# An up projection by seven block products in place of eight, in a phase of its own, in a hybrid encoder layer

## The chip, the cores and the metric

The kernel runs on one core of a Trainium2 chip. Times are device microseconds. Five engines work from queues of their own: PE (matmul; its weight loads are shown as PEld), DVE (vector), ACT (scalar), POOL (GpSimd), and SP, which here only issues DMAs. Semaphores order what depends on each other. The metric is the time of one execution; 2132.58 us is the median of three runs before the change (2130.88 to 2136.26).

## The reference

One layer, sequence 512, width 2048, all in f32:

```python
h = rms_norm(x, pre_mix_g)
proj = h @ w_in                                  # 2048 -> 1024 + 2 * 1024
y_ssm  = s5_mixer(u, ...)                        # diagonal state space, gelu, GLU
y_conv = conformer_conv_mixer(v, g, ...)         # causal depthwise conv of 31 taps
y = concatenate([y_ssm, y_conv]) @ w_out
x = x + rms_norm(y, post_mix_g)
h = rms_norm(x, pre_ffn_g)
up = causal_depthwise_conv(h @ w_up, conv_w)     # 2048 -> 2 * 5632, 3 taps
gate, val = split(up, 2)
f = (gelu(gate) * val) @ w_down                  # 5632 -> 2048
x = x + rms_norm(f, post_ffn_g)
```

The change is in the last four lines of matmul work: w_up, and the way from there to w_down.

## The kernel before

Everything is held with channels on the 128 partitions and the 512 time steps in the free dimension, so a row of tiles is 128 channels by 512. x has 16 such rows, gate and val 44 each.

**Products in three parts.** For f32 accuracy every weight tile and every activation is split into a high part, rounded to fp32r, and the low rest, and three matmuls are done for each block: high by high (L118), high weight by low activation (L119), low weight by high activation (L120). The right operands are `hl` (high and low of the normalised x). Weights come in pieces of 512 KB as 128x1024 f32 tiles `wraw` (three buffers), by DMAs that SP issues (L88); ACT casts each to `wh` (L98), DVE subtracts to get `wl` (L99), two buffers each. A piece serves 8 blocks, 24 matmuls of 512 columns. `gemm` does four output rows at a time in four PSUM banks of a pool `mm` of six.

**The stages.** Norm, W_in, state space and conv work, W_out (to about 640 us). Then the x-add stage, lines 677 to 698: per row of x, DVE multiplies the new part by the norm (L686, which reads the norm from the PSUM tile `aux`), adds x (L687), ACT makes the high part and DVE the low part of the next operand (L689), POOL adds up squares (L697); x+y goes to DRAM as `x1scr`, for it is needed again at the end.

**The FFN.** `up(i)` makes 2 rows of gate and 2 of val: 8 weight pieces, 192 matmuls; DVE evacuates PSUM times the norm `rr` into padded buffers `ab` (L720); per row of f, ACT does tap 0 (L728), DVE taps 1 and 2 (L730), ACT the gelu (L733), DVE the product of gate and val (L734), ACT and DVE the split into `hidh` and `hidl` (L736, L738), which stay in SBUF. `down(b)` takes four of these rows: 16 output rows, each accumulated in SBUF tiles `s` over the 11 calls (L755). 22 ups and 11 downs alternate. Before the last down, two DMAs of 2 MB bring x1 back (L774) into the `hl` tiles that the ups no longer need. `rsqrt_bcast` (L133, L146) sums squares over the partitions by matmuls of one column and spreads the result by matmuls with a diagonal.

**The order** on each engine is set by a scheduler that goes by program order and by priorities: weight loads and splits are raised by WPRI, evacuations by EPRI. Each engine, and SP's queue, then runs its list strictly in that order.

## Time and profile before

| | us |
|---|---|
| median of 3 runs | 2132.58 (2130.88 to 2136.26) |
| the profiled execution | 2129.79 |
| its span, first to last instruction | 2128.0 |
| PE busy in the span | 2012.5 (95%) |
| DVE, ACT, POOL busy | 1218.9, 666.3, 287.6 |

The span runs from the first to the last instruction of the profiled execution. "Busy" of PE counts pipelined matmuls, whose single times overlap; so the pitch, the time per instruction in a stretch without holes, is what counts there. Where an engine is idle the profile gives the instruction that ended the wait, after an arrow. In the first 700 us the engines take turns at being full, after that PE is busy nearly without a break until 2098 us; the mean granted TensorE clock is 0.976 of 2.4 GHz.

### The profile page before, as it was taken

The numbers are of one execution on the slowest core, as the hardware profiler recorded it, in microseconds if no ns is written. First come the engines' busy times: TensorE is split into PE (matmuls) and PEld (weight loads), VectorE is DVE, ScalarE is ACT, GpSimd is POOL, SyncE is SP. The second block draws the span as 40 slices with busy tenths as digits, with TensorE's granted clock in tenths as the row PEclk, the third lists the DMA queues.
The fourth block names the chain that finished last, engine by engine and source line by source line (L and its number), as shares of the span: only waits on it lengthen the run. The fifth ranks groups of instructions, "written<-read, shape, count | busy, mean of one in ns | idle before, by whom it ended". The sixth has DMA issues, their size and how long they took to land.

```text
span 2128.0 us, 23254 instructions
## 1 busy us (share of the span) xinstructions
PE 2012.5 (95%) x9190; PEld 1654.4 (78%) x9190; DVE 1218.9 (57%) x1609; ACT 666.3 (31%) x827; POOL 287.6 (14%) x291
## 2 busy tenths in 40 slices
...
GB/s 207 184 219 171 187 187 221 85 89 98 169 99 119 110 99 99 99 92 96 99 99 97 92 99 99 99 93 96 99 99 98 92 98 99 99 93 96 99 168 99
DMA packets 111373, 252.36 MB, mean 119 GB/s; under 512 B 28064, under 2 KB 49568, under 8 KB 110752
## 3 DMA queue, kind: packets, MB, share of 16 engines
...
q14 instruction: 37, 0.30, 0.0%
HBM read 229.67 MB, written 21.17 MB: 118 GB/s over the span
## 4 chain that ended last, share of the span: by engine, by line
PE 72%; DVE 3%; ACT 1%; issue 0%; DVEq 0%; ACTq 0%
PE mm L120 24%; PE mm L118 24%; PE mm L119 24%; DVE hl L689 0%; DVE s L779 0%; DVE s L686 0%; DVE wl L99 0%; DVE hidh L687 0%; PE aux L146 0%; DVE s L780 0%; DVE hidl L687 0%; ACT L139 0%; ACT wh L98 0%; ACT tmp L763 0%; ACT tmp L659 0%
## 5 line engine op out<-in xcount | busy, mean ns | idle before, releaser
L99 DVE TENSOR_TENSOR wl<-wraw,wh 128x1024 fp32r<-128x1024 f32 (+1 forms) x353 | 447.6, 1268 | 772.1 <-ACT wh L98 766.1
L118 PE MATMUL mm<-hl,wh 128*128 128x512 f32 x2112 | 832.7, 395 | 23.3 <-ACT wh L98 14.6
L119 PE MATMUL mm<-hl,wh 128*128 128x512 f32 x2112 | 831.8, 394 | 0.2 <-DVE hl L689 0.2
L120 PE MATMUL mm<-hl,wl 128*128 128x512 f32 x2112 | 777.5, 396 | 52.5 <-DVE wl L99 52.5
L98 ACT CAST wh<-wraw 128x1024 fp32r<-128x1024 f32 (+1 forms) x353 | 370.7, 1050 | 1077.6 <-PE mm L119 1006.3
L120 PEld LDWEIGHTS mm<-hl,wl 128*128 128x128 f32 x2112 | 402.5, 191 | 148.1 <-DVE wl L99 64.1
L118 PEld LDWEIGHTS mm<-hl,wh 128*128 128x128 f32 x2112 | 402.8, 191 | 108.6 <-ACT wh L98 15.4
L119 PEld LDWEIGHTS mm<-hl,wh 128*128 128x128 f32 x2112 | 402.7, 191 | 86.4 <-DVE hl L689 1.4
L119 PE MATMUL mm<-hidl,wh 128*128 128x512 f32 x704 | 273.8, 389 | 0.0
L118 PE MATMUL mm<-hidh,wh 128*128 128x512 f32 x704 | 273.2, 389 | 0.0
L120 PE MATMUL mm<-hidh,wl 128*128 128x512 f32 x704 | 252.6, 389 | 0.0
L765 POOL TENSOR_TENSOR ssq<-ssq,tmp 128x512 f32<-128x512 f32 x11 | 17.4, 1583 | 1380.6 <-ACT tmp L763 1380.0
L571 DVE SCALAR_TENSOR_TENSOR csb<-z,c_conv_w,csb 128x512 f32<-128x512 f32 x210 | 181.0, 920 | 0.0
L118 PEld LDWEIGHTS mm<-hidh,wh 128*128 128x128 f32 x704 | 132.1, 188 | 27.9 <-ACT wh L98 0.5
L120 PEld LDWEIGHTS mm<-hidh,wl 128*128 128x128 f32 x704 | 132.2, 188 | 27.5
L119 PEld LDWEIGHTS mm<-hidl,wh 128*128 128x128 f32 x704 | 132.1, 188 | 27.3
L755 DVE TENSOR_TENSOR s<-mm,s 128x512 f32<-128x512 f32 x160 | 109.3, 690 | 44.4 <-PE mm L120 44.2
L730 DVE SCALAR_TENSOR_TENSOR tmp<-ab,c_ffn_conv_w,tmp 128x512 f32<-128x512 f32 x176 | 125.3, 745 | 0.0
L728 ACT ACTIVATE tmp<-ab,c_ffn_conv_w 128x512 f32<-128x512 f32 x88 | 63.0, 719 | 44.5 <-DVE ab L720 44.5
L720 DVE TENSOR_TENSOR ab<-mm,rr 128x512 f32<-128x512 f32 x88 | 60.3, 688 | 8.2 <-PE mm L120 4.5
L568 POOL TENSOR_TENSOR csb<-csb,pt 128x512 f32<-128x512 f32 x30 | 49.3, 1645 | 60.4 <-ACT pt L567 60.4
L736 ACT CAST hidh<-tmp 128x512 fp32r<-128x512 f32 x44 | 27.2, 621 | 78.1 <-DVE tmp L734 78.1
...
## 6 DMA issues: line engine op xcount, KB each, us to landing
wraw<-in_ffn_w_up SPq DMA_DIRECT2D x176, 512.0 KB, 3.4
wraw<-in_ffn_w_down SPq DMA_DIRECT2D x88, 512.0 KB, 3.4
wraw<-in_w_in SPq DMA_DIRECT2D x47, 512.0 KB, 5.2
wraw<-in_w_out SPq DMA_DIRECT2D x32, 512.0 KB, 3.4
...
k<-in_ssm_bT SPq DMA_DIRECT2D x8, 512.0 KB, 3.7
...
```

The lines of the kernel that those rows point to most:

```text
L98: se.copy(out=h[:, o], in_=raw[:, o])
L99: ve.tensor_tensor(out=l[:, o], in0=raw[:, o], in1=h[:, o].bitcast(F32), op=SUB)
L118: pe.matmul(ps[m], wh[:, kk, m, :], xh, start=k == 0, stop=False)
L119: pe.matmul(ps[m], wh[:, kk, m, :], xl, start=False, stop=False)
L120: pe.matmul(ps[m], wl[:, kk, m, :], xh, start=False, stop=k == nk - 1)
L568: ge.tensor_tensor(out=csb[:, c, :], in0=csb[:, c, :], in1=pt, op=ADD)
L571: ve.scalar_tensor_tensor(out=csb[:, c, :], in0=zk, scalar=w, in1=csb[:, c, :], op0=MUL, op1=ADD)
L720: ve.tensor_tensor(out=t[:, 2:], in0=ps[j], in1=r2, op=MUL)
L728: se.activation(out=o, in_=t[:, 0:S], func=AF.Copy, scale=fcw[:, c, 0:1])
L730: ve.scalar_tensor_tensor(out=o, in0=t[:, k:k + S], scalar=fcw[:, c, k:k + 1], in1=o, op0=MUL, op1=ADD)
L736: se.copy(out=h, in_=cvt[0])
L755: ve.tensor_tensor(out=ft(m), in0=ps[i], in1=ft(m), op=ADD)
```

## The change

Four rows of f are made by `up` as before (`up(0)`, `up(1)`). For the other 40, w_up's part for one row is seen as a 2 by 2 matrix of blocks: gate or val (index 1 or 2) by lower or upper half of the contraction, each block a 128x1024 tile (w11, w12, w21, w22); h is 2 by 2 as well, contraction half by half of the 512 time steps. The product of two such matrices is made by seven block products in place of eight, after Winograd's form of Strassen's method. The sums of h are made once (`xsum` L757, `xsplit` L761 and L762): t1 = h12 - h11, t2 = h22 - t1, t3 = h22 - h12, t4 = h21 - t2. Those of the weights are made for each row: s1 = w21 + w22 and w11 - w21 on POOL (L805, L808), s1 - w11 and w12 less that on DVE (L841, L848). Each product is split (L787 on ACT, L788 on DVE) and run as 8 x 3 matmuls of 256 columns (L793 to L795). The partial sums are put together on their way from PSUM: two copies on ACT, five additions of 256 columns on DVE (L818, L822, L845, L853, L854); the multiplication by the norm (L819, L823) and that of gate and val (L732) are POOL's. A row's last two products, t4 and 22, are done after the first of the next row. `wh` and `wl` have three buffers.

f goes to DRAM (`fscr`, L733). After the whole up phase the down phase reads it back four rows at a time (`fload`: L876, cast L878, low part L880). For the sums, ACT makes a second scaled copy of all 16 rows of h in f32 (L702). The rows of x are loaded into tiles of their own. The reload of x1 is now L915.

```diff
+NP = 4
+HS = S // 2
...
+    for k in range(DK):
+        x1 = xip.tile([P, S], F32, name=f"xin{k}")
+        sy.dma_start(out=x1, in_=a["x"][:, k, :])
+        x1s.append(x1)
...
     x1scr = dram.tile([P, DK, S], F32, name="x1scr")
-    x1s = []
-    for k in range(DK):
-        x1 = hid.tile([P, S], F32, name="hidl" if k % 2 else "hidh")
-        sy.dma_start(out=x1, in_=a["x"][:, k, :])
-        x1s.append(x1)
+    fscr = dram.tile([P, NFF, S], F32, name="fscr")
...
     r2 = rsqrt_bcast([xs2], D)
...
+    for k in range(DK):
+        se.activation(out=yt(k), in_=x1s[k], func=AF.Copy, scale=g2[:, k:k + 1])
...
+    tset = [[xt.tile([P, 8, HS], F32R, name=f"t{i}{p}") for p in "hl"] for i in range(3)]
+    NA = 4
+    abuf = [xt.tile([P, S + 2], F32, name=f"ab{i}") for i in range(NA)]
...
+    def gated(f, ab, mul):
+        cvt = []
...
+            se.activation(out=o, in_=t[:, 0:S], func=AF.Copy, scale=fcw[:, c, 0:1])
+            for k in (1, 2):
+                ve.scalar_tensor_tensor(out=o, in0=t[:, k:k + S], scalar=fcw[:, c, k:k + 1], in1=o,
+                                        op0=MUL, op1=ADD)
+            cvt.append(o)
+        se.activation(out=cvt[0], in_=cvt[0], func=AF.Gelu_apprx_tanh)
+        mul.tensor_tensor(out=cvt[0], in0=cvt[0], in1=cvt[1], op=MUL)
+        sy.dma_start(out=fscr[:, f, :], in_=cvt[0])
...
                 ve.tensor_tensor(out=t[:, 2:], in0=ps[j], in1=r2, op=MUL)
             ab.append(t)
...
-            se.activation(out=cvt[0], in_=cvt[0], func=AF.Gelu_apprx_tanh)
-            ve.tensor_tensor(out=cvt[0], in0=cvt[0], in1=cvt[1], op=MUL)
-            h = hid.tile([P, S], F32R, name="hidh")
-            se.copy(out=h, in_=cvt[0])
-            l = hid.tile([P, S], F32R, name="hidl")
-            ve.tensor_tensor(out=l, in0=cvt[0], in1=h.bitcast(F32), op=SUB)
-            hrow.append((h, l))
+            gated(2 * i + f, ab[2 * f:2 * f + 2], ge)
+
+    up(0)
...
+    q11, q12 = yo[0][:, :, 0:HS], yo[0][:, :, HS:S]
+    q21, q22 = yo[1][:, :, 0:HS], yo[1][:, :, HS:S]
+    xset = {"11": (hh[0][:, :, 0:HS], hl_[0][:, :, 0:HS]), "21": (hh[1][:, :, 0:HS], hl_[1][:, :, 0:HS]),
+            "22": (hh[1][:, :, HS:S], hl_[1][:, :, HS:S]), "t4": (hh[0][:, :, HS:S], hl_[0][:, :, HS:S])}
+    for i in range(3):
+        xset[f"t{i + 1}"] = tuple(tset[i])
+
+    def xsum(name, dst, in0, in1):
+        ve.tensor_tensor(out=dst, in0=in0, in1=in1, op=SUB)
+
+    def xsplit(name, src):
+        h, l = xset[name]
+        se.copy(out=h, in_=src)
+        ve.tensor_tensor(out=l, in0=src, in1=h.bitcast(F32), op=SUB)
+
+    xsum("t1", q11, q12, q11)
+    xsplit("t1", q11)
+    xsum("t3", q12, q22, q12)
+    xsum("t2", q22, q22, q11)
+    xsplit("t2", q22)
+    xsplit("t3", q12)
+    xsum("t4", q21, q21, q22)
+    for i in range(1, NP // 2):
+        up(i)
+    xsplit("t4", q21)
+    s16x.close()
+
...
+    def product(raw, name, ps, first, last):
+        pool = sp if nw[0] % 3 == 2 else wp
+        nw[0] += 1
+        h = pool.tile([P, 1024], F32R, name="wh")
+        l = pool.tile([P, 1024], F32R, name="wl")
+        with tc.high_priority(offset=WPRI):
+            se.copy(out=h, in_=raw)
+            ve.tensor_tensor(out=l, in0=raw, in1=h.bitcast(F32), op=SUB)
+        h, l = (v.rearrange("p (k f) -> p k f", f=P) for v in (h, l))
+        xh_, xl_ = xset[name]
+        o = ps[:, 0:HS]
+        for k in range(8):
+            pe.matmul(o, h[:, k, :], xh_[:, k, :], start=first and k == 0, stop=False, skip_group_check=True)
+            pe.matmul(o, h[:, k, :], xl_[:, k, :], start=False, stop=False, skip_group_check=True)
+            pe.matmul(o, l[:, k, :], xh_[:, k, :], start=False, stop=last and k == 7, skip_group_check=True)
+
+    def quad_load(f):
+        src = a["ffn_w_quad"][f - NP]
+        with tc.high_priority(offset=WPRI):
+            w21 = sp.tile([P, 1024], F32, name="rb", bufs=4)
+            sy.dma_start(out=w21, in_=src[2])
+            w22 = sp.tile([P, 1024], F32, name="rb", bufs=4)
+            sy.dma_start(out=w22, in_=src[3])
+            s1 = sp.tile([P, 1024], F32, name="s1", bufs=2)
+            ge.tensor_tensor(out=s1, in0=w21, in1=w22, op=ADD)
+            w11 = wp.tile([P, 1024], F32, name="wraw", bufs=3)
+            sy.dma_start(out=w11, in_=src[0])
+            ge.tensor_tensor(out=w21, in0=w11, in1=w21, op=SUB)
+            w12 = wp.tile([P, 1024], F32, name="wraw", bufs=3)
+            sy.dma_start(out=w12, in_=src[1])
+        return w11, w12, w21, w22, s1
+
+    def quad_end(f, st_):
+        (w11, w12, w21, w22, s1), ab, (px, py, pz) = st_
+        gate, val = ab
+        product(w22, "t4", py, False, True)
+        with tc.high_priority(offset=EPRI):
+            ve.tensor_tensor(out=val[:, 2:2 + HS], in0=py[:, 0:HS], in1=val[:, 2:2 + HS], op=ADD)
+            ge.tensor_tensor(out=val[:, 2:], in0=val[:, 2:], in1=r2, op=MUL)
+        product(w12, "22", pz, False, True)
+        with tc.high_priority(offset=EPRI):
+            ve.tensor_tensor(out=gate[:, 2 + HS:], in0=pz[:, 0:HS], in1=gate[:, 2 + HS:], op=ADD)
+            ge.tensor_tensor(out=gate[:, 2:], in0=gate[:, 2:], in1=r2, op=MUL)
+        gated(f, ab, ge)
+
+    before = None
+    for f in range(NP, NFF):
+        ws = quad_load(f)
+        w11, w12, w21, w22, s1 = ws
+        ab = [anext(), anext()]
+        gate, val = ab
+        px = psm.tile([P, S], F32, name="mm")
+        product(w11, "11", px, True, False)
+        with tc.high_priority(offset=EPRI):
+            se.copy(out=val[:, 2:2 + HS], in_=px[:, 0:HS])
+        if before:
+            quad_end(f - 1, before)
+        pz = psm.tile([P, S], F32, name="mm")
+        product(s1, "t1", pz, True, False)
+        with tc.high_priority(offset=WPRI):
+            ve.tensor_tensor(out=s1, in0=s1, in1=w11, op=SUB)
+        py = psm.tile([P, S], F32, name="mm")
+        product(s1, "t2", py, True, False)
+        with tc.high_priority(offset=EPRI):
+            ve.tensor_tensor(out=gate[:, 2 + HS:], in0=py[:, 0:HS], in1=val[:, 2:2 + HS], op=ADD)
+        product(w12, "21", px, False, True)
+        with tc.high_priority(offset=WPRI):
+            ve.tensor_tensor(out=w12, in0=w12, in1=s1, op=SUB)
+        with tc.high_priority(offset=EPRI):
+            se.copy(out=gate[:, 2:2 + HS], in_=px[:, 0:HS])
+        product(w21, "t3", py, False, False)
+        with tc.high_priority(offset=EPRI):
+            ve.tensor_tensor(out=val[:, 2 + HS:], in0=py[:, 0:HS], in1=val[:, 2:2 + HS], op=ADD)
+            ve.tensor_tensor(out=val[:, 2 + HS:], in0=pz[:, 0:HS], in1=val[:, 2 + HS:], op=ADD)
+        before = (ws, ab, (px, py, pz))
+    quad_end(NFF - 1, before)
+    spx.close()
...
+    def fload(b):
+        r = []
+        for i in range(4):
+            t = hid.tile([P, S], F32, name="fin", bufs=6)
+            sy.dma_start(out=t, in_=fscr[:, 4 * b + i, :])
+            h = hid.tile([P, S], F32R, name="hidh")
+            se.copy(out=h, in_=t)
+            l = hid.tile([P, S], F32R, name="hidl")
+            ve.tensor_tensor(out=l, in0=t, in1=h.bitcast(F32), op=SUB)
+            r.append((h, l))
+        return r
+
+    def down(b, rhs):
         for g in range(4):
-            ps = gemm(a["ffn_w_down"][b, g], hrow[4 * b:4 * b + 4])
+            ps = gemm(a["ffn_w_down"][b, g], rhs)
...
-    for i in range(NFF // 2):
-        up(i)
-        if i >= 2 and i % 2 == 0:
-            down(i // 2 - 1)
-    x1r = [hl16.tile([P, 8, S], F32, name="hl") for _ in range(2)]
-    for i in range(2):
-        sy.dma_start(out=x1r[i], in_=x1scr[:, 8 * i:8 * i + 8, :])
-    down(NB - 1)
+    nxt = fload(0)
+    for b in range(NB):
+        rhs = nxt
+        if b + 1 < NB:
+            nxt = fload(b + 1)
+        if b == NB - 1:
+            x1r = [hl16.tile([P, 8, S], F32, name="hl") for _ in range(2)]
+            for i in range(2):
+                sy.dma_start(out=x1r[i], in_=x1scr[:, 8 * i:8 * i + 8, :])
+        down(b, rhs)
...
+    r["ffn_w_quad"] = wu.reshape(2, 8, P, 2, NFF, P).transpose(4, 3, 0, 2, 1, 5)[NP:].reshape(NFF - NP, 4, P, 8 * P)
```

On DVE, one stretch of an up phase before: `wl` are weight splits, `ab` evacuated rows, `tmp` convolution results, `hid` the operands for down.

```order
L730 SCALAR_TENSOR_TENSOR tmp_9051<-ab1_5215,c_ffn_conv_w_472,tmp_9051 128x512
L99 TENSOR_TENSOR wl_9112<-wraw_9109,wh_9111 128x1024
L730 SCALAR_TENSOR_TENSOR tmp_9061<-ab2_5216,c_ffn_conv_w_472,tmp_9061 128x512
L734 TENSOR_TENSOR tmp_9047<-tmp_9047,tmp_9051 128x512
L730 SCALAR_TENSOR_TENSOR tmp_9065<-ab3_5217,c_ffn_conv_w_472,tmp_9065 128x512
L730 SCALAR_TENSOR_TENSOR tmp_9061<-ab2_5216,c_ffn_conv_w_472,tmp_9061 128x512
L730 SCALAR_TENSOR_TENSOR tmp_9065<-ab3_5217,c_ffn_conv_w_472,tmp_9065 128x512
L738 TENSOR_TENSOR hidl_9059<-tmp_9047,hidh_9057 128x512
L99 TENSOR_TENSOR wl_9142<-wraw_9139,wh_9141 128x1024
L734 TENSOR_TENSOR tmp_9061<-tmp_9061,tmp_9065 128x512
L738 TENSOR_TENSOR hidl_9073<-tmp_9061,hidh_9071 128x512
L99 TENSOR_TENSOR wl_9172<-wraw_9169,wh_9171 128x1024
```

Splits stand one by one between the work on the two rows of f that the last `up` has made.

And in the change, one row of f (s1, rb, wraw: weight blocks or their sums):

```order
L845 TENSOR_TENSOR ab0_5231<-mm_10970,ab1_5232 128x256
L788 TENSOR_TENSOR wl_11073<-wraw_11066,wh_11072 128x1024
L788 TENSOR_TENSOR wl_11102<-rb_10830,wh_11101 128x1024
L853 TENSOR_TENSOR ab1_5232<-mm_10970,ab1_5232 128x256
L854 TENSOR_TENSOR ab1_5232<-mm_10940,ab1_5232 128x256
L788 TENSOR_TENSOR wl_11132<-wraw_10837,wh_11131 128x1024
L788 TENSOR_TENSOR wl_11174<-s1_11064,wh_11173 128x1024
L841 TENSOR_TENSOR s1_11064<-s1_11064,wraw_11066 128x1024
L818 TENSOR_TENSOR ab1_5232<-mm_10970,ab1_5232 128x256
L788 TENSOR_TENSOR wl_11204<-s1_11064,wh_11203 128x1024
L822 TENSOR_TENSOR ab0_5231<-mm_10940,ab0_5231 128x256
L788 TENSOR_TENSOR wl_11233<-wraw_11069,wh_11232 128x1024
```

The splits are seven per row of f where they were four, two combinations (L841, L848) and the five short evacuations join them; the product and the low part of f are gone from here, the four convolution steps (L728, most of them in the rows left out) are the same.

On POOL before, nothing stands between the x-add stage (L697) and the last call of down (L765). In the change, these five repeat for every one of the 40 rows of f:

```order
L805 TENSOR_TENSOR s1_8512<-rb_8508,rb_8510 128x1024
L808 TENSOR_TENSOR rb_8508<-wraw_8514,rb_8508 128x1024
L819 TENSOR_TENSOR ab1_5232<-ab1_5232,rr_5203 128x512
L823 TENSOR_TENSOR ab0_5231<-ab0_5231,rr_5203 128x512
L732 TENSOR_TENSOR tmp_8377<-tmp_8377,tmp_8381 128x512
```

Two operations on weights, two on evacuated rows (`ab`), one on f now stand in one queue; the first two are for the row two after the one to which the others belong.

On SP before, the reload of x1 into `hl` behind the last weights of up:

```order
L88 DMA wraw_13927<-in_ffn_w_up 128x1024
L88 DMA wraw_13957<-in_ffn_w_up 128x1024
L774 DMA hl_14019<-x1scr_5029 128x4096
L774 DMA hl_14020<-x1scr_5029 128x4096
L88 DMA wraw_14027<-in_ffn_w_down 128x1024
L88 DMA wraw_14057<-in_ffn_w_down 128x1024
L88 DMA wraw_14109<-in_ffn_w_down 128x1024
```

Weights of down come after it, and nothing of f passes this queue.

And in the change, at the end of the up phase (`fin` is f coming back):

```order
L733 DMA fscr_5054<-tmp_14873 128x512
L90 DMA wraw_15206<-in_ffn_w_down 128x1024
L90 DMA wraw_15236<-in_ffn_w_down 128x1024
L915 DMA hl_18070<-x1scr_5053 128x4096
L915 DMA hl_18071<-x1scr_5053 128x4096
L90 DMA wraw_15274<-in_ffn_w_down 128x1024
L876 DMA fin_15086<-fscr_5054 128x512
L876 DMA fin_15092<-fscr_5054 128x512
L876 DMA fin_15098<-fscr_5054 128x512
L733 DMA fscr_5054<-tmp_15064 128x512
L876 DMA fin_15104<-fscr_5054 128x512
```

The reload stands behind four weight pieces of down, and ahead of the fifth and of the first loads of f; the store of the last row of f (L733) is among these loads.

## Rows read from the trace of the kernel before

**Rows 1.** Windows: busy us and instructions per engine, clock, DMA share, GB/s.
```profile
650.00:700.00 50.00, 42.32 (x165) 32.43 (x164) 49.33 (x54) 25.47 (x38) 23.46 (x15) 0.90 0.39 137
1200.00:1400.00 200.00, 200.00 (x884) 165.66 (x883) 83.93 (x97) 48.23 (x53) 0.00 (x0) 1.00 0.30 98
2100.00:2128.00 28.00, 5.94 (x33) 4.96 (x31) 20.36 (x37) 5.68 (x9) 10.30 (x8) 0.63 0.39 150
```

**Rows 2.** Page, costliest groups: busy, mean ns; idle before, its releaser.
```profile
L120 PE MATMUL mm<-hl,wl 128*128 128x512 f32 x2112 | 777.5, 396 | 52.5 <-DVE wl L99 52.5
```

**Rows 3.** Groups by form, 860 to 2100 us: DVE and ACT.
```profile
L99 DVE TENSOR_TENSOR wl<-wraw,wh 128x1024 fp32r<-128x1024 f32 x227 | 278.8, 1228 | 611.3 <-ACT wh L98 611.3
...
L98 ACT CAST wh<-wraw 128x1024 fp32r<-128x1024 f32 x227 | 239.3, 1054 | 770.5 <-PE mm L119 770.5
...
L730 DVE SCALAR_TENSOR_TENSOR tmp<-ab,c_ffn_conv_w,tmp 128x512 f32<-128x512 f32 x152 | 108.5, 745 | 0.0
...
L728 ACT ACTIVATE tmp<-ab,c_ffn_conv_w 128x512 f32<-128x512 f32 x76 | 54.7, 719 | 40.3 <-DVE ab L720 40.3
...
L733 ACT ACTIVATE tmp<-tmp 128x512 f32<-128x512 f32 x38 | 23.6, 621 | 0.0
```

**Rows 4.** Groups by form, whole span: POOL.
```profile
L697 POOL TENSOR_TENSOR ssq<-ssq,tmp 128x512 f32<-128x512 f32 x15 | 23.5, 1564 | 48.9 <-ACT tmp L696 48.8
...
L244 POOL TENSOR_TENSOR cf<-cf,cx 128x256 f32<-128x256 f32 x2 | 1.5, 731 | 0.0
...
L244 POOL TENSOR_TENSOR k<-k,sm_coi 128x512 f32<-128x512 f32 x1 | 1.1, 1062 | 0.0
```

**Rows 5.** Timeline, x-add stage: DVE (start, us, line, names).
```profile
655.06 1.41 DVE L687 TENSOR_TENSOR hidh<-hidh,s 128x512 f32<-128x512 f32 x1
...
657.05 0.67 DVE L686 TENSOR_TENSOR s<-s,aux 128x512 f32<-128x512 f32 x1
...
658.25 1.78 DVE L689 SCALAR_TENSOR_TENSOR hl<-hidh,c_pre_ffn_g,hl 128x512 fp32r<-128x512 f32 x1
...
672.39 2.32 DVE L99 TENSOR_TENSOR wl<-wraw,wh 128x1024 fp32r<-128x1024 f32 x1
```

**Rows 6.** Timeline, the same stretch: POOL.
```profile
654.64 1.28 POOL L697 TENSOR_TENSOR ssq<-ssq,tmp 128x512 f32<-128x512 f32 x1 [28.70 <-ACT tmp L696]
657.89 1.60 POOL L697 TENSOR_TENSOR ssq<-ssq,tmp 128x512 f32<-128x512 f32 x1 [1.97 <-ACT tmp L696]
...
672.03 1.60 POOL L697 TENSOR_TENSOR ssq<-ssq,tmp 128x512 f32<-128x512 f32 x1 [1.97 <-ACT tmp L696]
```

**Rows 7.** Chain that ended last: start, share of the chain in us.
```profile
656.47 0.66 DVE hl L689
657.13 0.60 DVE s L686
...
667.09 1.14 DVE wl L99
...
700.31 0.79 PE aux L133 x8
...
706.93 0.89 PE aux L146 x8
```

**Rows 8.** DMA issues: KB each, median us to landing; then line L88's own.
```profile
wraw<-in_ffn_w_down SPq DMA_DIRECT2D x88, 512.0 KB, 3.4
...
hl<-x1scr SPq DMA_DIRECT2D x2, 2048.0 KB, 11.9
...
DMA to landing us min/median/max: 3.3/3.4/11.1
```

**Rows 9.** Windows round an idle stretch of PE, columns as in rows 1.
```profile
97.90:109.50 11.60, 0.00 (x0) 0.00 (x0) 4.87 (x8) 0.13 (x1) 0.00 (x0) 0.60 1.03 207
109.50:115.50 6.00, 5.97 (x17) 4.79 (x18) 6.00 (x10) 0.23 (x1) 0.00 (x0) 0.64 1.19 224
115.50:120.00 4.50, 4.50 (x75) 3.74 (x74) 0.92 (x2) 1.98 (x3) 0.05 (x1) 1.00 1.04 410
```

More of the change, by code (lines that the diff above doesn't have):

```diff
@@ L123, in layer_kernel @@
     gpre = cload("pre_mix_g", [P, DK], se)
-    ones = const.tile([P, P], F32, name="ones")
+    ones = constr.tile([P, P], F32, name="ones")
     ge.memset(ones, 1.0)
@@ L698, in layer_kernel @@
     r2 = rsqrt_bcast([xs2], D)
-    fa = [s16.tile([P, 8, S], F32, name="s16") for _ in range(2)]
-    def ft(m):
-        return fa[m // 8][:, m % 8, :]
-    NA = 6
-    abuf = [t2.tile([P, S + 2], F32, name=f"ab{i}", bufs=1) for i in range(NA)]
+    for k in range(DK):
+        se.activation(out=yt(k), in_=x1s[k], func=AF.Copy, scale=g2[:, k:k + 1])
+    xin.close()
+    upx = ExitStack()
+    xt = upx.enter_context(tc.tile_pool(name="xt", bufs=1, reuse_waits="tile"))
+    tset = [[xt.tile([P, 8, HS], F32R, name=f"t{i}{p}") for p in "hl"] for i in range(3)]
+    NA = 4
+    abuf = [xt.tile([P, S + 2], F32, name=f"ab{i}") for i in range(NA)]
     for t in abuf:
@@ L710, in layer_kernel, with anext @@
     na = [0]
-    hrow = []
+    def anext():
+        t = abuf[na[0] % NA]
+        na[0] += 1
+        return t
+    def gated(f, ab, mul):
+        cvt = []
+        for j in range(2):
+            c = f + NFF * j
+            t = ab[j]
+            o = tmp()
+            se.activation(out=o, in_=t[:, 0:S], func=AF.Copy, scale=fcw[:, c, 0:1])
[6 more added lines that the diff above has]
+        sy.dma_start(out=fscr[:, f, :], in_=cvt[0])
     def up(i):
@@ L716, in up @@
         for j in range(4):
-            t = abuf[na[0] % NA]
-            na[0] += 1
+            t = anext()
             with tc.high_priority(offset=EPRI):
```

50 lines of the change are left out of this document (24 added, 26 removed).

## The prediction

> **What bounds the kernel now.** I read the table of windows first. From 700 us on PE has no hole: in 1200 to 1400 it is busy 200.00 of 200 us with 884 matmuls, one per 0.2262 us, at granted clock 1.00, while DVE stands at 83.93, ACT at 48.23 and POOL at nothing [rows 1]. So in the FFN only the number and pitch of the matmuls count: a row of f (gate and value, 96 matmuls of 512 columns) is 96 x 0.2262 = 21.72 us, and the down part is 2112 x 0.2262 = 477.8 us. Before 700 us other engines rule, in 650 to 700 DVE (49.33 of 50 us); after 2100 PE is nearly idle [rows 1]. The list of groups says the same: of PE's waits the largest is 52.5 us for wl in 2112 matmuls [rows 2]; a busy 200 of 200 leaves none of it to the later FFN. The profiled execution took 2129.79 us, its span 2128.0, so 1.8 us lie around the span; it is 2.8 us below the median of 2132.58.
>
> **The change part by part.**
>
> *Products.* Rows 0 to 3 of f keep the old form. Each of the other 40 becomes 7 x 8 x 3 = 168 matmuls of 256 columns: 7/8 of the columns, but 1.75 times the instructions and weight loads. No 256-column matmul stands in the trace. Half of 0.2262 is 0.113, which is the low end. Of the 0.2262, 0.2133 is 512 columns at 2.4 GHz; if the other 0.013 is per instruction, a half is 0.1067 + 0.013 = 0.120. Does the weight load fit under it? The chain shows eight matmuls of one column, each with its own 128x128 load, in 0.79 us, and eight of 128 columns of f32 in 0.89 [rows 7]: at most 0.11 each, and the load bound is as good as independent of what streams beside it, so load and stream overlap. If they did not, 0.1067 + 0.11 = 0.22 would be the other end. I take 0.120: 168 x 0.120 = 20.2 us per row on PE (18.8 at 0.112), against 21.72.
>
> The Trainium skill ("TensorE: Matmul & The Clock Gate", Back-to-back issue gap) gives columns/2.4 + 2.5 ns, so an estimate of 109 ns here and 18.3 us per row. The trace's 512-column pitch is 226 ns where that rule gives 216, so I stay with rows.
>
> *What DVE and POOL get.* This is the term that decides. Per row DVE has 7 splits L788 and 2 combinations (L841, L848) of 1024 columns, 4 convolution steps of 512 and 5 PSUM evacuations of 256. In back-to-back work a 1024 split takes 1.14 us of the chain and a 512 STT 0.66 [rows 7]; means of single ones are 1.228 and 0.745 [rows 3]. So 9 x 1.14 + 4 x 0.66 = 12.9 us read two SBUF operands, and the evacuations are 5 x 0.34 = 1.7 us (half of the 0.68 us that L686, which reads PSUM, stands for [rows 5]; pitch 0.60 [rows 7]). Alone, 14.6 us would be covered by PE. But POOL, idle here before, gets five operations per row: L805 and L808 of 1024 columns and L819, L823, L732 of 512. An undisturbed 512 takes 1.06 us; for 1024 twice that is 2.12, and going on by the slope from the 256 one (0.73) gives 1.06 + 2 x 0.33 = 1.72 [rows 4]; I take the middle, 1.93. Together 2 x 1.93 + 3 x 1.06 = 7.0 us.
>
> The two don't run beside each other. In the x-add stage L687 took 1.41 us and L689 1.78 next to POOL instructions of 1.28 and 1.60, L99 even 2.32, while L686, with one SBUF operand, kept its 0.67 in the same stretch [rows 5, 6]; and POOL's own mean there is 1.564 against 1.06 alone [rows 4]. So two-operand DVE work and POOL work add: 12.9 + 7.0 = 19.9 us per row, with the evacuations beside POOL where one falls on a POOL operation. I count half of them as not covered: 19.9 + 0.85 = **20.8 us per row**, which is just above PE's 20.2. That, not the matmuls, sets the period. If all evacuations fall well and nothing waits, PE sets 20.2; if none does, and DVE also waits for ACT casts with POOL having nothing to do, 22.5 (rival below). ACT has seven casts of 1.05, two activations of 0.72, a gelu of 0.62 and two copies of 256 columns (under 0.4 each), about 10 us [rows 3]; the four 512 KB loads per row land in 3.4 us each in a period of 20 [rows 8]. Gain: 40 x (21.72 - 20.8) = **-37 us**.
>
> The Trainium skill ("GPSIMD Engine Reference", Elementwise — side-by-side cycle accounting) gives 4497 ns for a two-input add of 2048 elements, by proportion an estimate of 2.25 us at 1024. No row shows a 1024; by that figure the sum is 0.64 us larger and the period 21.4, which gives 2144.
>
> *x-add stage and first rows.* ACT gets 16 scaled copies, 16 x 0.72 = 11.5 us [rows 3], where it is half busy (25.47 of 50 [rows 1]); DVE, which bounds the stage, gets one combination of 2048 columns in it, 2 x 1.14 = 2.3 us, and seven more operations of that width (three combinations, four low parts) during rows 0 to 3, where it has room. The broadcast of the second norm now stands behind a weight split that is behind these in DVE's order, so that evacuation of the first tiles starts later, and with six PSUM buffers PE waits in the second block: I put 5 us on that, 0 to 10. Sum **+7** (2 to 12). Starting the block products costs some 3 us while combinations and splits come at once (0 to 8): **+3**.
>
> *From up to down.* Up and down alternate before, and hid rows are in SBUF; now f goes to DRAM and back. On SP the reload of x1 (two of 2 MB) is moved ahead of the loads of f. Its first half waits for the last t4 product (some 2.7 us before the end T of up), its second for the very last matmul; then one weight load, then f. Two of them landed 11.9 us after issue, about 6 us each, and the weight load behind them took 11.1 in place of 3.4 [rows 8]: the queue goes in order. So first half until T + 3.3, second T + 9.3, weights 1.5 more, f 0.8 more at the same rate: T + 11.6, then the cast of 0.62 [rows 3]. PE idle 12.2 us. After an idle stretch of 11.6 us PE's granted clock was 0.64 over the next 6 us, i.e. mostly 1.2 GHz, before 1.00 came back [rows 9]: +2. Sum **+14**. Without the reload in front, evacuation, multiplication, convolution, gelu and cast of the last row still come to some 6 us: range 8 to 20. The down part keeps its 2112 matmuls, and its splits are covered as before. The tail is the same.
>
> **Sum.** 2128.0 + 7 + 3 - 37 + 14 = 2115 span; + 1.8 around it = 2116.8; + 2.8 for a median rather than this one execution: **2120 us**, 0.6% faster. The break-even period is 21.72 - 24/40 = 21.1 us. No change means within 0.3% (6.4 us), about what a measurement of this kernel can tell.
>
> **Rivals.**
> - *PE sets the period.* DVE and POOL interlock without loss, for 19.9 is below 20.2. 40 x 1.52 = 61 in place of 37: 2096; with 0.112 per matmul 40 x 2.92 = 117: 2040. For it: the evacuations can run beside POOL, as L686 does. Against it: the two engines would have to be 99% full together, while DVE's order is strict and alternates with waits for casts.
> - *The pair DVE and POOL serialises with holes (slower).* Nothing runs beside POOL's work, 12.9 + 1.7 + 7.0 = 21.6, and a hole of 0.9 us per row, DVE at the head of its queue waiting for a cast while splits that could go stand behind it. Period 22.5: +31 in place of -37, 2188. It decides against the change from 21.1 us on. For it: L99 took 2.32 and L689 1.78 wherever POOL is active [rows 5]; POOL multiplications L819 and L823 stand between an evacuation and the convolution, so PE's banks and DVE's queue both wait for them. Against it: POOL's combinations are issued two rows ahead.
> - *POOL's wide operations cost what two 512 cost.* 2 x (2.12 - 1.93) = 0.4 more per row, period 21.2, 2136: no change. For it: a POOL instruction has shown no fixed part that two would share, beyond the slope of one pair of sizes [rows 4]. The Trainium skill's proportion ("GPSIMD Engine Reference", above) goes further the same way.
> - *Weight loads show.* At 256 columns load and stream are nearly equal; any extra above 0.126 us per matmul (21.1/168) makes the change slower; at 0.130, 21.84 per row, 2161. Against it are the eight-matmul rows [rows 7].
> - *The gain at the turn is lost less.* The DMA in front of f costs only 6 us: 2112, inside the forecast's range.
>
> **How the numbers follow.** Forecast (period 20.4 to 21.1) 0.38, own range 2105 to 2135; PE sets the period 0.24, of which 0.06 for the lower pitch; POOL's wide operations 0.08; serialised pair with holes 0.22; weight loads 0.05; others (start-up or turn cost much more) 0.03. Faster: 0.28 of the forecast and all 0.24 of PE: 0.52. Same: 0.08 of the forecast, 0.06 of POOL's wide operations, 0.02 of the serialised pair: 0.16. Slower: the rest, 0.32. The range 2070 to 2185 leaves out the low pitch and the far end of the serialised pair, under 2 in 10.
>
> **What would show it.** In the up phase: the start of one 11 product to the next about 20.8 us; PE at 97% there, DVE near 90% and POOL near 45% with its 512 operations above 1.4 us; PE's waits on wl of L788. PE at 100% with 0.112 to 0.120 per matmul and periods of 20.2 or less says rival one; periods above 21.1 with DVE and POOL alternating say rival two; matmul pitch above 0.126 with no waits says rival three. At the turn one hole of 12 us ended by the load of f. The forecast is wrong if POOL's 1024 instruction takes well over 2 us or DVE does not slow beside it.

## The result and the profile after

The change makes the kernel slower: 2229.26 us median (2227.70 to 2231.20, 4 runs) against 2132.13 us, a ratio of 1.0458 (95% interval 1.0445 to 1.0471). The forecast was 2120, the range ended at 2185. The profiled execution has a span of 2225.9 us, 97.9 more than before. (One of the four executions of the experiment e1 below took 3812 us and stands outside all its numbers; the other three took 2114.1 to 2116.5.) By stages, before and after each taken from the trace:

| stage | before | after | difference | forecast |
|---|---|---|---|---|
| to the norm ahead of the x-add stage | 643.2 | 647.0 | +3.8 | 0 |
| x-add stage and rows 0 to 3 of f | 109.2 | 121.2 | +12.0 | +7 |
| 40 rows of f | 868.8 | 935.2 | +66.4 | -37 + 3 |
| hole at the turn | 0 | 14.4 | +14.4 | +12 |
| down's 2112 matmuls | 477.8 | 481.3 | +3.5 | +2 |

(868.8 and 477.8 are counts of matmuls by the pitch of [rows 1]. The stages differ by 100.1 in sum, the spans by 97.9: in the trace of before, rows and down took 3.0 us longer than this count, and what follows down is 0.8 us longer after. The first line shows no effect: the same stretch ended at 641.7 to 647.6 us in the experiments, which change nothing ahead of it.) All that went wrong with the sign is in the third line: a row of f takes 23.4 us, not 20.8 (40 x 23.37 are 934.8 of the 935.2, so the 3 us for starting the block products did not come).

Windows of the profile after: steady part of the up phase, the turn, the stretch behind it, and the down phase (columns as in [rows 1]):

```profile
860.00:1560.00 700.00, 634.07 (x5032) 615.06 (x5032) 621.17 (x540) 280.04 (x360) 318.56 (x150) 0.99 0.30 102
1703.40:1717.80 14.40, 0.02 (x2) 0.01 (x1) 4.91 (x7) 3.61 (x6) 2.35 (x2) 0.58 0.99 385
1717.80:1723.00 5.20, 5.20 (x13) 4.10 (x14) 4.34 (x7) 3.91 (x7) 0.00 (x0) 0.53 0.90 310
1723.00:2100.00 377.00, 377.00 (x1665) 312.17 (x1664) 187.45 (x226) 98.67 (x118) 0.00 (x0) 1.00 0.36 120
```

5032 matmuls in 700 us are 29.95 rows of 168, so 23.37 us each. No engine is full: PE is busy 634 of 700, DVE 621, POOL 319, where before PE stood at 200 of 200 [rows 1]. PE's waits in the same 700 us (engine, operation, what ended the wait: us in total, times, longest):

```profile
PE mm L793 <- DVE ab L845: 42.7, 30, 1.5
PE mm L795 <- DVE wl L788: 15.0, 17, 0.9
PE mm L793 <- ACT wh L787: 6.4, 18, 0.5
```

That is 64 us in 30 rows, 2.1 per row. By the distance of the matmuls the holes cost more, 97 us in the window or 3.2 per row, which is all that a row takes above 168 matmuls of 0.12: the profile counts the first part of a hole as busy, and behind 82 of the 83 holes (matmuls over 0.3 us apart) the first matmul is followed after 0.22 us and not 0.12. DVE, by groups:

```profile
L788 DVE TENSOR_TENSOR wl<-wraw,wh 128x1024 fp32r<-128x1024 f32 x90 | 147.4, 1638 | 2.3
L788 DVE TENSOR_TENSOR wl<-s,wh 128x1024 fp32r<-128x1024 f32 x60 | 122.8, 2047 | 68.1 <-ACT wh L787 68.1
L841 DVE TENSOR_TENSOR s<-s,wraw 128x1024 f32<-128x1024 f32 x30 | 95.3, 3177 | 1.0
...
L788 DVE TENSOR_TENSOR wl<-rb,wh 128x1024 fp32r<-128x1024 f32 x60 | 72.7, 1212 | 0.0
L848 DVE TENSOR_TENSOR wraw<-wraw,s 128x1024 f32<-128x1024 f32 x30 | 60.0, 1999 | 1.0
...
L818 DVE TENSOR_TENSOR ab<-mm,ab 128x256 f32<-128x256 f32 x30 | 12.4, 413 | 0.0
```

A free 1024-column operation on DVE takes 1.212 us (splits of rb, with nothing on POOL beside them), near the 1.228 of [rows 3]. The same on wraw takes 1.638 in the mean, on s 2.047, L841 3.177, L848 1.999. The additions that read PSUM (L818) keep their 0.41. POOL's groups and the bounds of one of them:

```profile
L808 POOL TENSOR_TENSOR rb<-wraw,rb 128x1024 f32<-128x1024 f32 x30 | 95.5, 3183 | 7.6 <-DMA wraw<-in_ffn_w_quad 5.8
L805 POOL TENSOR_TENSOR s<-rb 128x1024 f32<-128x1024 f32 x30 | 81.1, 2704 | 169.6 <-DMA rb<-in_ffn_w_quad 169.6
L823 POOL TENSOR_TENSOR ab<-ab,rr 128x512 f32<-128x512 f32 x30 | 59.8, 1993 | 28.1 <-DVE ab L822 28.1
L819 POOL TENSOR_TENSOR ab<-ab,rr 128x512 f32<-128x512 f32 x30 | 44.5, 1485 | 26.9 <-DVE ab L818 26.9
L732 POOL TENSOR_TENSOR tmp<-tmp 128x512 f32<-128x512 f32 x30 | 38.5, 1284 | 150.4 <-ACT ab L850 140.3 <-ACT wh L787 10.0
```

```profile
L805 POOL TENSOR_TENSOR s<-rb x40: 2394/2404/3484, 756.7 to 1656.6; 128x1024 f32<-128x1024 f32 x40
```

The shortest wide sum takes 2.394 us, half of them no more than 2.404; the forecast had 1.93. The narrow ones have 1.09 at best, near the 1.06 of [rows 4]. The means are longer because POOL is held up as well. How the two engines block each other, in the timeline of one row, DVE first, then POOL:

```profile
1001.76 3.27 DVE L788 TENSOR_TENSOR wl<-s,wh 128x1024 fp32r<-128x1024 f32 x1 [1.42 <-ACT wh L787]
1005.06 3.31 DVE L841 TENSOR_TENSOR s<-s,wraw 128x1024 f32<-128x1024 f32 x1
1008.29 0.41 DVE L818 TENSOR_TENSOR ab<-mm,ab 128x256 f32<-128x256 f32 x1
1009.56 1.40 DVE L788 TENSOR_TENSOR wl<-s,wh 128x1024 fp32r<-128x1024 f32 x1 [0.85 <-ACT wh L787]
```

```profile
1001.54 2.40 POOL L805 TENSOR_TENSOR s<-rb 128x1024 f32<-128x1024 f32 x1 [5.51 <-DMA rb<-in_ffn_w_quad]
1004.02 3.27 POOL L808 TENSOR_TENSOR rb<-wraw,rb 128x1024 f32<-128x1024 f32 x1
```

L788 starts 0.2 us behind L805 and ends 1.1 us after it; L808, issued meanwhile, then takes its 2.3 us from there; L841 ends 1.1 us after that. L805 and L788 together last 3.5 us, where one after the other they would take 2.40 + 1.22. What [rows 5, 6] showed once for an operation or two is here a chain of four. Behind L841 and L818 DVE waits 0.85 us for the cast of the new sum by ACT.

### The profile page after: what moved, and what is told of

It is laid out like the page before. It is cut to its first block, busy times and chain, and to the rows that moved or that the text cites. A ratio compares the mean times of both kernels' runs of the same rounds, so it can differ in the third digit from the quotient of the medians.

```text
span 2225.9 us, 30245 instructions
## 1 busy us (share of the span) xinstructions
PE 1997.7 (90%) x12070; PEld 1761.6 (79%) x12070; DVE 1688.0 (76%) x1893; ACT 811.2 (36%) x1047; POOL 725.6 (33%) x493
## 4 chain that ended last, share of the span: by engine, by line
PE 37%; DVE 20%; issue 7%; ACT 3%; DMA 0%; ACTq 0%; DVEq 0%; SPq 0%
PE mm L120 8%; PE mm L122 8%; PE mm L121 8%; DVE wl L788 7%; PE mm L793 5%; PE mm L794 4%; PE mm L795 4%; DVE s L841 4%; ACT wh L787 3%; DVE tmp L728 3%; DVE wraw L848 3%; DVE ab L822 1%; DVE ab L845 1%; DMA fin<-fscr 0%; DVE fa L920 0%
## 5 line engine op out<-in xcount | busy, mean ns | idle before, releaser
L101 DVE TENSOR_TENSOR wl<-wraw,wh 128x1024 fp32r<-128x1024 f32 (+1 forms) x193 | 254.6, 1320 | 245.5 <-ACT wh L100 239.5
L100 ACT CAST wh<-wraw 128x1024 fp32r<-128x1024 f32 (+1 forms) x193 | 201.6, 1046 | 508.8 <-PE mm L121 458.3
L122 PE MATMUL mm<-hl,wl 128*128 128x512 f32 x832 | 316.0, 412 | 64.5 <-DVE wl L101 64.5
L793 PE MATMUL mm<-hl,wh 128*128 128x256 f32 x1280 | 366.1, 286 | 5.7 <-ACT wh L787 5.1
L795 PE MATMUL mm<-hl,wl 128*128 128x256 f32 x1280 | 362.2, 283 | 0.0
L794 PE MATMUL mm<-hl,wh 128*128 128x256 f32 x1280 | 362.1, 283 | 0.0
L120 PE MATMUL mm<-hl,wh 128*128 128x512 f32 x832 | 333.6, 405 | 20.6 <-ACT wh L100 12.5
L121 PE MATMUL mm<-hl,wh 128*128 128x512 f32 x832 | 332.7, 402 | 0.2 <-DVE hl L691 0.2
L120 PE MATMUL mm<-hidh,wh 128*128 128x512 f32 x704 | 274.9, 391 | 14.4 <-ACT hidh L878 14.4
L793 PEld LDWEIGHTS mm<-hl,wh 128*128 128x128 f32 x1280 | 245.6, 192 | 10.8 <-ACT wh L787 7.3
L795 PEld LDWEIGHTS mm<-hl,wl 128*128 128x128 f32 x1280 | 245.8, 192 | 0.0
L788 DVE TENSOR_TENSOR wl<-s,wh 128x1024 fp32r<-128x1024 f32 x80 | 162.2, 2028 | 89.1 <-ACT wh L787 89.1
L788 DVE TENSOR_TENSOR wl<-wraw,wh 128x1024 fp32r<-128x1024 f32 x120 | 194.4, 1620 | 7.4 <-ACT wh L787 4.6
L787 ACT CAST wh<-s 128x1024 fp32r<-128x1024 f32 x80 | 83.8, 1048 | 281.0 <-DVE s L841 169.1
L805 POOL TENSOR_TENSOR s<-rb 128x1024 f32<-128x1024 f32 x40 | 106.1, 2653 | 231.1 <-DMA rb<-in_ffn_w_quad 231.1
```

Of the source, the lines that this page charges most:

```text
L100: se.copy(out=h[:, o], in_=raw[:, o])
L101: ve.tensor_tensor(out=l[:, o], in0=raw[:, o], in1=h[:, o].bitcast(F32), op=SUB)
L120: pe.matmul(ps[m], wh[:, kk, m, :], xh, start=k == 0, stop=False)
L121: pe.matmul(ps[m], wh[:, kk, m, :], xl, start=False, stop=False)
L122: pe.matmul(ps[m], wl[:, kk, m, :], xh, start=False, stop=k == nk - 1)
L787: se.copy(out=h, in_=raw)
```

## The experiments

Theory A: DVE's operations with two SBUF operands are held up by POOL instructions. Theory B: it is the chain from one product's weights to the next, with three buffers and DVE's strict order, whoever holds what.

**e1, e2, e3: work moved from POOL to DVE.** e1 the wide sums, e3 the narrow operations, e2 all:

```diff
-            ge.tensor_tensor(out=s1, in0=w21, in1=w22, op=ADD)
+            ve.tensor_tensor(out=s1, in0=w21, in1=w22, op=ADD)
...
-            ge.tensor_tensor(out=w21, in0=w11, in1=w21, op=SUB)
+            ve.tensor_tensor(out=w21, in0=w11, in1=w21, op=SUB)
```

```diff
-            ge.tensor_tensor(out=val[:, 2:], in0=val[:, 2:], in1=r2, op=MUL)
+            ve.tensor_tensor(out=val[:, 2:], in0=val[:, 2:], in1=r2, op=MUL)
...
-            ge.tensor_tensor(out=gate[:, 2:], in0=gate[:, 2:], in1=r2, op=MUL)
+            ve.tensor_tensor(out=gate[:, 2:], in0=gate[:, 2:], in1=r2, op=MUL)
-        gated(f, ab, ge)
+        gated(f, ab, ve)
```

> The two wide sums of weights (1024 columns, L805 and L808) go from POOL to DVE, nothing else. Theory A (POOL's wide instructions keep DVE's two-operand instructions waiting for their whole length): DVE gains 2 x 1.14 us of work per row of f and loses about 4.2 us of waiting; the period falls from 23.4 to 20.3 to 21.2 us, near PE's 20.2, and the time to 2105 to 2145 us. Theory B (the chain from t1 over s1 - w11 to t2 is limited by three weight buffers and by the strict order of DVE's queue, whoever holds a port): the period stays at 22.5 to 23.5, the time at 2195 to 2235.

> All five POOL operations of a row of f go to DVE. DVE's own work is then 12.9 + 2.3 + 1.7 + 3 x 0.66 = 18.9 us per row, below PE's 20.2. Theory A: PE sets the period, 20.2 to 20.6, time 2100 to 2120, about the same as with the wide ones alone or a little less. Theory B: DVE's queue gets longer, the chain through it as well, period 23 or more, time 2215 to 2260.

> Only the three 512-column operations (L819, L823, L732) go to DVE, the wide ones stay on POOL. Theory A: the wide instructions are the main part; the two engines' sum falls by 3 x (1.08 - 0.66) = 1.3 us and the wide ones still hold DVE for 2 x 2.3: period 21.8 to 22.8, time 2165 to 2205. Theory B: period 23 or more, time above 2215. If the narrow ones were the main cause, it would fall below 2145 here and not with the wide ones moved.

Measured: e1 2116.5 us (ratio to before 0.9925, 0.9906 to 0.9945), e2 2125.8 (0.9970, 0.9959 to 0.9981), e3 2152.6 (1.0101, 1.0086 to 1.0116). e1 came out as A says. DVE has more work and yet the kernel is 113 us faster than the change. The window of e1:

```profile
860.00:1560.00 700.00, 698.34 (x5796) 696.17 (x5795) 647.48 (x691) 329.48 (x414) 208.76 (x104) 1.00 0.35 117
```

5796 matmuls, 20.29 us per row, PE nearly without a hole. e3 fell further than either theory had it, so the narrow ones count too. e2 is slower than e1, and above the range that A gave, although POOL does nothing there; its period is 20.70 us and PE waits again for casts by ACT (11.2 us in the window). Why, was not settled: DVE stands idle 1.6 us per row.

**e5 and e12: POOL as busy, but reading nothing.** The wide sums replaced by two (e5) or three (e12) memsets each; both kernels leave the sums out of the computation:

```diff
-            ge.tensor_tensor(out=s1, in0=w21, in1=w22, op=ADD)
+            for _ in range(3):
+                ge.memset(s1, 0.0)
...
-            ge.tensor_tensor(out=w21, in0=w11, in1=w21, op=SUB)
+            for _ in range(3):
+                ge.memset(w21, 0.0)
```

> The changed kernel with the two wide sums of weights on POOL left out of the computation: in place of each stand two POOL memsets over the same 1024 columns, which write but read nothing and together take about as long (448 columns took 0.47 us, so some 2.1 us for two). POOL stays as occupied, and t1's operand as late as before. Theory A (DVE's operations with two SBUF operands are held up by POOL instructions that read SBUF): DVE's stalls at L788 and L841 go, DVE 14.6 + narrow POOL 3.3 = 17.9 us is below PE's 20.2, period 20.2 to 20.7, time 2095 to 2125. Theory B (POOL being late or busy at all, and the chain through three buffers): period 22.5 to 23.5, time 2195 to 2235.

> As e5, the wide sums left out of the computation, with three memsets in place of each: 3 x 0.955 = 2.87 us, more than the 2.40 us of a wide sum on POOL, so that POOL is busier per row than in the changed kernel and t1's operand comes later. If POOL's reading of SBUF is what holds DVE, the period stays at 20.1 to 20.5 and the time at 2100 to 2115. If in e5 the shorter POOL work (1.91 for 2.40) was what helped, the period is back above 22 and the time above 2170.

Measured: e5 2102.4 us (0.9869, 0.9855 to 0.9884), e12 2099.2 (0.9852, 0.9835 to 0.9868). e12's window, its POOL memsets, and a stretch of one row on POOL and then on DVE:

```profile
860.00:1560.00 700.00, 700.00 (x5836) 700.00 (x5835) 595.24 (x624) 334.67 (x417) 313.69 (x306) 1.00 0.35 118
```

```profile
L810 POOL MEMSET rb<- 128x1024 f32 x102 | 97.4, 955 | 47.8 <-DMA rb<-in_ffn_w_quad 43.9
L806 POOL MEMSET s<- 128x1024 f32 x99 | 94.5, 954 | 85.1 <-DVE wraw L850 81.3
```

```profile
1017.47 2.98 POOL L806 MEMSET s<- 128x1024 f32 x3 [2.46 <-DVE wraw L850]
1021.27 1.30 POOL L732 TENSOR_TENSOR tmp<-tmp 128x512 f32<-128x512 f32 x1 [0.82 <-ACT tmp L731]
```

```profile
1017.26 2.07 DVE L728 SCALAR_TENSOR_TENSOR tmp<-ab,c_ffn_conv_w,tmp 128x512 f32<-128x512 f32 x3
1019.25 1.22 DVE L788 TENSOR_TENSOR wl<-rb,wh 128x1024 fp32r<-128x1024 f32 x1
...
1021.38 2.26 DVE L788 TENSOR_TENSOR wl<-wraw,wh 128x1024 fp32r<-128x1024 f32 x1
```

POOL works 2.87 us for each sum, more than the 2.40 of the change, and PE has no hole. Beside the memsets DVE keeps its times: three convolution steps in 2.07 us, then a split in 1.22; right behind, beside a product of 512 columns that reads (L732), a split takes 2.26. In the window of e12, 100 splits with a memset beside them for most of their time took 1.21 to 1.23 us, 105 beside a POOL instruction that reads 1.40 to 2.27. So it is not POOL's time that costs.

Nor is it the lateness of POOL's results. e12 alone does not show that, for there the memsets of s wait for a free buffer and not for a load; but in the trace of the change itself no wait is put down to L805, and only one of 0.3 us to L808. What costs is that POOL's instruction works on SBUF inputs while DVE reads two operands there. A memset lacks the inputs and the arithmetic on them, and no run sets one without the other beside such a split, so that it is the reading is not shown by these runs alone. The Trainium skill states it of the reading ("SBUF — State Buffer", Who interferes with whom): two SBUF inputs on DVE contend with a GpSimd instruction that reads SBUF, not with one that only writes. The two groups of splits in e12 agree with it.

**e9, e10, e11: is it a sum, or the order?** After e1 to e5 I made a rule of theory A: the period is DVE's own work plus POOL's own. e9 moves only L808, e10 only L823 to DVE (the lines above). e11 moves nothing between engines, but puts the convolution behind the evacuation L845 (`quad_end` gives `ab` back and no longer calls `gated`):

```diff
...
-        if before:
-            quad_end(f - 1, before)
+        done = quad_end(f - 1, before) if before else None
...
-            ve.tensor_tensor(out=gate[:, 2 + HS:], in0=py[:, 0:HS], in1=val[:, 2:2 + HS], op=ADD)
+            e845 = ve.tensor_tensor(out=gate[:, 2 + HS:], in0=py[:, 0:HS], in1=val[:, 2:2 + HS], op=ADD).ins
+        if done:
+            with tc.issue_after(e845):
+                gated(f - 1, done, ge)
...
```

> Only the second wide sum (L808) goes to DVE. Theory A, now as a rule with numbers (the period is DVE's own work plus POOL's own work, or PE's 20.2 if that is more; own times 1.14, 0.66, 0.34 on DVE and 2.40, 1.09 on POOL): 15.7 + 5.7 = 21.4 us, with up to 0.7 of holes as in the changed kernel 22.1; time 2150 to 2180. If either wide one alone makes the chain late (the limit is a latency, not a sum): still above 22.8, time above 2200.

> Only the multiplication of gate by the norm (L823, 512 columns) goes to DVE. Rule of the sum: 15.3 + 7.0 = 22.3 us, with holes up to 23.0; time 2185 to 2215. If instead this one operation, waiting on POOL for its turn, makes the convolution late and with it the evacuation L845 behind it in DVE's order (PE's hole of 1.45 us in each row), the hole goes with it and the period is 22.0 or less: 2160 to 2180.

> The changed kernel with the convolution steps (L728) put behind the evacuation L845 in DVE's order; nothing moves between engines. Rule of the sum: work is the same, 22.7 us and holes; period 22.7 to 23.4, time 2200 to 2230. If the strict order is what costs PE its 1.45 us hole in each row, the period falls to 22.0 and the time to 2165 to 2185.

Measured: e9 2130.7 us (0.9997, 0.9987 to 1.0006), e10 2146.8 (1.0071, 1.0056 to 1.0086), e11 2175.1 (1.0206, 1.0189 to 1.0223). All three lie below what the rule of the sum gives: it fell. The sum is not even a lower bound: e10 has 22.3 us of work on the two engines in a period of 21.32. e11 came out as its second case says and shows 54 us for order alone. PE's waits in e11, where L845 is L844, and the first in e10:

```profile
PE mm L793 <- ACT wh L787: 26.2, 16, 2.5
PE mm L795 <- DVE wl L788: 5.3, 10, 1.4
PE mm L793 <- DVE ab L844: 4.0, 7, 0.6
```

```profile
PE mm L793 <- DVE ab L845: 18.1, 33, 0.6
```

The wait for L845 goes from 1.42 us per row to 0.13 in e11 (4.0 us in 31.7 rows), where waits for casts rise from 0.21 to 0.83, and to 0.55 in e10 (18.1 in 32.8). Why L845 is late, in the row of the change shown above:

```profile
1011.43 1.94 POOL L823 TENSOR_TENSOR ab<-ab,rr 128x512 f32<-128x512 f32 x1 [1.56 <-DVE ab L822]
```

```profile
1013.41 1.34 ACT L726 ACTIVATE tmp<-ab,c_ffn_conv_w 128x512 f32<-128x512 f32 x2 [2.94 <-POOL ab L823]
```

```profile
1012.46 2.00 DVE L848 TENSOR_TENSOR wraw<-wraw,s 128x1024 f32<-128x1024 f32 x1
1014.38 2.06 DVE L728 SCALAR_TENSOR_TENSOR tmp<-ab,c_ffn_conv_w,tmp 128x512 f32<-128x512 f32 x3
...
1018.16 0.41 DVE L845 TENSOR_TENSOR ab<-mm,ab 128x256 f32<-128x256 f32 x1
```

L823 takes 1.94 us here for 1.09, held up by DVE's work as DVE is by it; in the 30 rows of the window it takes 1.94 to 2.08, and in 12 of them it also starts 0.4 us later, behind L819. So ACT's and DVE's convolution come late, and L845 stands behind them. The table has the steady periods (860 to 1560 us; own work by the prices of the forecast, with 2.40 and 1.09 for POOL; held: DVE's busy time less its own work):

| kernel | period | DVE own | POOL own, reading | DVE held | DVE idle |
|---|---|---|---|---|---|
| change | 23.37 | 14.6 | 8.1 | 6.1 | 2.6 |
| e11 order | 22.08 | 14.6 | 8.1 | 4.9 | 2.6 |
| e3 narrow on DVE | 21.42 | 16.6 | 4.8 | 4.0 | 0.9 |
| e10 L823 on DVE | 21.32 | 15.3 | 7.0 | 4.1 | 1.9 |
| e9 L808 on DVE | 20.87 | 15.7 | 5.7 | 4.1 | 1.1 |
| e2 all on DVE | 20.70 | 18.9 | 0 | 0.2 | 1.6 |
| e1 wide on DVE | 20.29 | 16.9 | 3.3 | 1.9 | 1.5 |
| e12 memsets | 20.15 | 14.6 | 3.3 | 2.5 | 3.0 |

POOL's reading holds DVE for 0.58 to 0.83 of its length (the columns held and POOL own), by what stands in DVE's order at that moment. DVE's idle time is no measure of the loss by itself: where PE is full, as in e12, it costs nothing.

**e4: phases only.** All rows by the old up, the rest as in the change:

```diff
-    for i in range(1, NP // 2):
+    for i in range(NFF // 2):
         up(i)
...
-    before = None
-    for f in range(NP, NFF):
...
-    quad_end(NFF - 1, before)
```

> All 44 rows of f by the old up (eight block products as 96 matmuls of 512), product of gate and val on DVE, no sums of h and no second copy of it; what stays of the change is the up phase, then the down phase with f in DRAM. By the trace of the changed kernel the turn costs 14.4 us and some 3 us of half clock behind it: time 2143 to 2155. If the split into phases also loses cover for other work, more than 2165; if the hole at the turn is a matter of the block products, within 6 us of before.

Measured: 2143.5 us (1.0059, 1.0044 to 1.0074). PE's one wait at the turn is 10.0 us here. The split into phases is a small part of the loss, some 12 us of 97.

**e6, e7, e8: the two other terms, and a better kernel.** On top of e1: e6 the reload of x1 behind the last load of f, e7 the sums of h behind the first evacuations of up, e8 both (`fl[0]` is the last load of f issued, `ev0` the last evacuation of `up(0)`):

```diff
...
-            for i in range(2):
-                sy.dma_start(out=x1r[i], in_=x1scr[:, 8 * i:8 * i + 8, :])
+            with tc.issue_after(fl[0]):
+                for i in range(2):
+                    sy.dma_start(out=x1r[i], in_=x1scr[:, 8 * i:8 * i + 8, :])
...
     def xsum(name, dst, in0, in1):
-        ve.tensor_tensor(out=dst, in0=in0, in1=in1, op=SUB)
+        with tc.issue_after(ev0):
+            ve.tensor_tensor(out=dst, in0=in0, in1=in1, op=SUB)
```

> The wide sums on DVE as in e1, and the reload of x1 put behind the last load of f on SP's queue, near the end of the down phase. If the two 2 MB transfers ahead of the first f make the hole at the turn (14.7 us in e1), it falls to 6 to 8 us and the time to 2105 to 2112. If the hole is made by the chain of the last row (evacuation, multiplication, convolution, gelu, store, load, cast), it stays at 13 to 15 and the time at 2113 to 2119.

> The wide sums on DVE as in e1, and the four sums and splits of h put behind the evacuation of the first up in DVE's order, in place of ahead of the second norm's broadcast. If these 2048-column operations in front of the norm make PE wait there (holes of 4.75 and 1.4 us and parts of the 6.0 us one), the stretch before the block products shrinks by 5 to 11 us: 2105 to 2112. If the stage is held by ACT's second copies of h (16 x 0.71 us), it stays: 2113 to 2119.

> Wide sums on DVE, reload of x1 late, sums of h late together. If the three terms are independent: 2229 - 113 - 7 - 7 = about 2102 (2095 to 2108), 1.4% below the kernel before. If the gain at the start only moves the wait to the first block products: 2107 to 2113.

Measured: e6 2114.6 us (0.9922, 0.9905 to 0.9939), e7 2108.0 (0.9893, 0.9873 to 0.9912), e8 2101.0 (0.9861, 0.9838 to 0.9884). In e6 PE's wait at the turn is

```profile
PE mm L120 <- ACT hidh L880: 7.6, 1, 7.6
```

in place of 14.7 in e1, as expected; but the time fell by 2 us only, for its 40 rows took 830.9 us, those of e1 825.0, with the same order on DVE, ACT, POOL and PE. The two ran on different chips, but e7 and e8, on the chip of e6, took 826.8 and 822.8; what makes these 6 us was not settled, so e6's expectation held for the hole and not for the time. e7 gained 8.5 us, though its runs spread from 2103.6 to 2112.9; in its trace the x-add stage and the first rows take 113.2 us for the 121.3 of e1. e8 is 31 us faster than the kernel before, and 128 faster than the change as it was made.

## Why the prediction was wrong

**Matmul pitch: right.** 0.120 us was taken; e12 has 5836 in 700 us, 0.1199, and the 109 ns that stand beside it in the prediction were not reached. The pitch stays under the 0.126 of the rival of the weight loads, so that is out. Whether the stream or the load sets the 0.12 no run tells: both are busy in all 700 us. PE's 20.15 us per row, 63 us less for 40 rows, is what e5 and e12 came to (without the sums), and e1 nearly (20.29).

**POOL and two-operand DVE work don't run together: right,** as the two groups of splits in e12 and the timeline of one row show.

**The period of 20.8: wrong, the step that failed.** Two things in it. First, the price of POOL's 1024-column operation: 1.93 by the middle of two bounds, 2.40 measured, above the upper bound of 2.12; that is 0.9 us per row. The prediction had named this as a sign that it is wrong. The Trainium skill's figure ("GPSIMD Engine Reference", Elementwise — side-by-side cycle accounting), 2.25 as an estimate, was nearer, though still low. Second, the sum took DVE and POOL as a pair that is never idle, with half of the evacuations in POOL's shadow. In the trace DVE's own 14.6 us was right (e2, with POOL empty, has 0.2 more than its own work by the same prices), but it is held 6.1 us and stands idle 2.6: each blocked split or sum makes a cast, a convolution step or an evacuation late, and what could go stands behind it. With 2.40 in place of 1.93 the forecast's sum would have been 21.7 us per row and 2157 us, slower already; the other 1.6 us are order and waiting, of which e11 gives back 1.3 without moving work (by the table 1.2 us of the time that DVE is held, and none of its idle time).

**Which rival it was.** The serialised pair with holes, which had 0.22, is nearest to what happened. It had 21.6 + 0.9 = 22.5; the true price of the wide sums turns this into 23.4. That the total agrees so well is in part luck: 2.0 of POOL's 8.1 us held nothing up, where the rival has nothing beside POOL's work, and DVE stood idle 2.6 us, not 0.9. Its argument "against", that the sums are issued two rows ahead, was no help: not their lateness costs, but what they hold up.

**x-add stage and first rows: +12 for +7.** The mechanism was named, its size not. DVE in the changed kernel, ahead of up's second block:

```profile
717.03 0.15 DVE L138 TENSOR_SCALAR rs<-aux 128x4 f32<-128x4 f32 x1
717.11 2.27 DVE L757 TENSOR_TENSOR s<-s 128x2048 f32<-128x2048 f32 x1
719.31 2.27 DVE L762 TENSOR_TENSOR t1l<-s,t1h 128x2048 fp32r<-128x2048 f32 x1
721.51 1.21 DVE L101 TENSOR_TENSOR wl<-wraw,wh 128x1024 fp32r<-128x1024 f32 x1
722.64 0.16 DVE L142 RECIPROCAL rs<-rs 128x4 f32<-128x4 f32 x1
...
727.92 2.48 DVE L741 TENSOR_TENSOR ab<-mm,rr 128x512 f32<-128x512 f32 x4 [4.53 <-ACT rr L152]
```

The norm's reciprocal (L142) comes 5.6 us after its first step (L138), behind two 2048-column operations and a split, and the evacuation (L741) 11 us after. The first step itself stands behind four more operations of that width. In e7, which puts these sums later, the reciprocal follows the first step by 0.4 us, and the time is 8.5 us less.

**The turn: right in size and in the main way.** 14.4 us and a lower clock behind it (granted 0.53 in the 5.2 us after, 1.00 from then on) for 12.2 + 2. The chain through it:

```profile
1703.33 1.05 ACT wh L100
1704.41 1.82 DVE wl L101
1706.25 0.33 SPq L90
1706.63 10.47 DMA fin<-fscr
1717.12 0.63 ACT hidh L878
1717.79 2.08 PE mm L120 x4
```

One detail was missed: the first load of f is issued 3 us after PE's end, since SP stands at a weight load (L90) that waits for a buffer, until the piece in it is cast (L100) and split (L101). The load lands 10.5 us after its issue and 13.7 after PE's end, for the forecast's 11.6. In e6, without the reload in front of it, it lands 3.6 us after its issue.
